# Gate and up of 18 of 22 column tiles by seven products of halves instead of eight, in both FFNs of an encoder block

## The chip, the cores and the metric

The kernel runs on one core of one Trainium2 chip. The metric is the device time of one execution in microseconds, as the median of several runs. A core has TensorE (PE, matrix products; PEld is its weight load), VectorE (DVE), ScalarE (ACT), GpSimd (POOL) and SyncE (SP, which issues the DMAs here). They run side by side, each in its own order, and wait for each other by semaphores.

## The reference, cut to what matters

One encoder block on 512 tokens and 16 meta tokens (528 rows) of width 1024: a SwiGLU FFN, a mixing stage (a gated linear recurrence beside attention), and a second SwiGLU FFN on the 512 tokens that are left.

```python
def swiglu(x, w_gate, w_up, w_down):
    return (jax.nn.silu(x @ w_gate) * (x @ w_up)) @ w_down
...
h = h + 0.5 * swiglu(rms_norm(h, ffn1_norm), ffn1_w_gate, ffn1_w_up, ffn1_w_down)
...   # mixing
h = h + 0.5 * swiglu(rms_norm(h, ffn2_norm), ffn2_w_gate, ffn2_w_up, ffn2_w_down)
```

The inner width of both FFNs is 2816, which is 22 column tiles of 128. All of it is float32.

## The kernel before, in words

Everything is held transposed: a tile has 128 features on the partitions and the tokens along the free dimension. `h` is 8 such tiles (width 1024). A float32 operand of a big product is split in two parts of the type float32r, `hi` (a rounded copy, made by ACT) and `lo` (the rest, made by a DVE subtraction), and a product is three matmuls: hi·hi, hi·lo, lo·hi (`group`, line 143). One matmul has a 128x128 block of weights as its stationary side and up to 512 tokens as its moving side.

`Weights` (line 51) brings the weights in the order of one long plan. `emit` loads one block (128x1024, 512 KB) by a DMA from SP, and writes `whi` (ACT, line 75) and `wlo` (DVE, line 76). There are two buffers of `raw`, two of `whi` and two of `wlo`; `fill` has at most three blocks traced ahead of the one that PE uses.

`ffn` (line 254) goes through the column tiles in three groups of 8, 8 and 6. For each tile it makes the gate and the up product over all 8 blocks of the width; DVE multiplies both by `R`, the reciprocal root of the mean square of each token (lines 265 and 268), which comes late in FFN1; ACT takes the silu (266), DVE multiplies (269), and ACT and DVE split the result into `hh` and `hl` (220 and 221). At the end of a group come eight "down" products of the group's tiles, each added to one tile of `h` (283). In FFN1 the 528 tokens go as 256 and 272 into two PSUM banks, in FFN2 as 512 into one; `parts` (197) deals the banks `mm` (three), `at`, `am` and the wide `S` in turn. The moving side of gate and up is `xt`, the 8 tiles of `h` times the norm's gain, split into `xh` and `xl`.

Outside of the mixing stage a planner orders the instructions of each engine: of those whose inputs and buffers its own model has ready, the one traced first goes first. A tile's buffer is taken again when the last reader of the old content is done. `gap` (208) puts unused bytes between tiles, which moves the addresses of those after it.

## Time and profile before

| | us |
|---|---|
| median of 3 runs (1236.92 to 1238.35) | 1238.31 |
| the profiled execution | 1237.46 |
| its span, first to last instruction | 1235.6 |
| PE busy | 1205.9 (98%) |
| DVE busy | 679.7 (55%) |
| ACT busy | 438.5 (35%) |
| POOL busy | 135.0 (11%) |
| mean granted clock of TensorE, of full speed | 0.994 |

FFN1 takes the span up to about 399 us, the mixing stage up to about 878 us, FFN2 the rest. Busy times of an engine are the time in which it had an instruction in work; matmuls are pipelined, so their ends are modelled and the durations of one matmul overlap those of the next. The pace of PE is read from the time that a row of equal matmuls took.

### The profile page before, as it was taken

To read this page: it belongs to the slowest core of one execution; us is meant where nothing else is said; L and a number is where in the kernel's file an instruction comes from. 1 tells how busy PE (TensorE), PEld (TensorE's weight loads), DVE (VectorE), ACT (ScalarE), POOL (GpSimd) and SP (SyncE) were. 2 spreads that over 40 slices of the span, in tenths; PEclk is the share of its full clock that TensorE was granted. 3 is DMA by queue.
4 is the path that set the end of the run, shared out by engine and by line. 5 is a ranking of instruction groups with operands and counts; after the bars stand their busy time and mean duration, and the time that the engine had idled before them with its cause. 6 is when DMAs were issued, how large, how long until landed. Compare 5 with 4: busy or idle time off the path is not lost.

```text
span 1235.6 us, 17678 instructions
## 1 busy us (share of the span) xinstructions
PE 1205.9 (98%) x7333; PEld 1078.1 (87%) x7333; DVE 679.7 (55%) x1082; ACT 438.5 (35%) x650; POOL 135.0 (11%) x122
## 2 busy tenths in 40 slices
PE   8999999999999998989889999999999999999998
PEld 8999999999999887878778788888888888888887
DVE  6544344433455879888698845454544334443443
ACT  5322122312235464555436533334323223222321
POOL 1000000000002114333142410122000000000000
PEclk9999999999999999999999999999999999999999
DMA  4232232223323311102111113233232332332223
GB/s 175 86 99 90 86 104 99 88 86 90 99 70 102 102 59 52 54 27 69 32 55 36 52 52 100 89 117 96 95 102 86 102 95 93 102 102 89 99 86 119
DMA packets 31919, 106.09 MB, mean 86 GB/s; under 512 B 3680, under 2 KB 4064, under 8 KB 31840
## 3 DMA queue, kind: packets, MB, share of 16 engines
q1 hardware_dynamic: 31680, 104.44, 26.6%
q8 instruction: 57, 0.93, 0.3%
q0 software_dynamic: 160, 0.54, 0.1%
q14 instruction: 22, 0.18, 0.0%
HBM read 102.87 MB, written 2.10 MB: 85 GB/s over the span
## 4 chain that ended last, share of the span: by engine, by line
PE 89%; DVE 7%; issue 1%; ACT 1%; DMA 0%; POOL 0%; SPq 0%; DVEq 0%; ACTq 0%; POOLq 0%
PE mm L151 49%; PE am L151 11%; PE at L151 11%; PE S L151 10%; PE gs L699 2%; PE mm L753 1%; PE mm L547 1%; PE S L509 1%; PE at L532 1%; DVE Z L688 1%; DVE aq L374 0%; DVE nm L513 0%; DVE wlo L76 0%; DVE pl L536 0%; DMA h<-in_xT 0%
## 5 line engine op out<-in xcount | busy, mean ns | idle before, releaser
L75 ACT CAST whi<-raw 128x1024 fp32r<-128x1024 f32 (+2 forms) x204 | 202.8, 994 | 571.1 <-PE mm L151 257.1
L151 PE MATMUL mm<-xh,whi 128*128 128x512 f32 (+1 forms) x872 | 270.9, 349 | 7.5 <-DVE tm L358 2.2
L151 PE MATMUL mm<-xh,wlo 128*128 128x512 f32 (+1 forms) x872 | 264.2, 342 | 0.3 <-DVE wlo L76 0.3
L151 PE MATMUL mm<-xl,whi 128*128 128x512 f32 (+1 forms) x872 | 263.6, 341 | 0.4 <-DVE xl L227 0.3
L76 DVE TENSOR_TENSOR wlo<-raw,whi 128x1024 fp32r<-128x1024 f32 (+2 forms) x204 | 235.3, 1154 | 27.6 <-ACT whi L75 22.7
L151 PEld LDWEIGHTS mm<-xh,whi 128*128 128x128 f32 x872 | 152.4, 190 | 26.7 <-DVE tm L358 2.6
L151 PEld LDWEIGHTS mm<-xh,wlo 128*128 128x128 f32 x872 | 151.7, 189 | 19.4 <-DVE wlo L76 0.8
L151 PEld LDWEIGHTS mm<-xl,whi 128*128 128x128 f32 x872 | 151.9, 189 | 16.3 <-DVE xl L227 0.8
L151 PE MATMUL mm<-hl,whi 128*128 128x512 f32 (+1 forms) x212 | 64.0, 340 | 0.1
L151 PE MATMUL mm<-hh,whi 128*128 128x512 f32 (+1 forms) x212 | 63.9, 339 | 0.0
L151 PE MATMUL mm<-hh,wlo 128*128 128x512 f32 (+1 forms) x212 | 63.9, 339 | 0.0
L686 POOL TENSOR_TENSOR Z<-Z,tot 128x512 f32<-128x512 f32 x32 | 46.2, 1442 | 152.8 <-PE gs L699 123.2
L151 PE MATMUL at<-xl,whi 128*128 128x256 f32 (+1 forms) x192 | 62.5, 326 | 0.0
L151 PE MATMUL at<-xh,wlo 128*128 128x256 f32 (+1 forms) x192 | 62.5, 326 | 0.0
L151 PE MATMUL at<-xh,whi 128*128 128x256 f32 (+1 forms) x192 | 62.5, 326 | 0.0
L151 PE MATMUL am<-xl,whi 128*128 128x272 f32 (+1 forms) x184 | 60.6, 329 | 0.0
L151 PE MATMUL am<-xh,wlo 128*128 128x272 f32 (+1 forms) x184 | 60.2, 327 | 0.0
L151 PE MATMUL am<-xh,whi 128*128 128x272 f32 (+1 forms) x184 | 60.1, 327 | 0.0
L283 DVE SCALAR_TENSOR_TENSOR h<-mm,h 128x512 f32<-128x512 f32 (+2 forms) x29 | 15.8, 565 | 64.5 <-PE mm L151 64.5
L268 DVE TENSOR_TENSOR u<-mm,R 128x512 f32<-128x512 f32 (+2 forms) x28 | 14.5, 541 | 63.8 <-PE mm L151 63.8
L151 PE MATMUL S<-xh,whi 128*128 128x256 f32 x224 | 45.8, 285 | 0.0
L238 POOL TENSOR_TENSOR acc<-acc,sq 128x528 f32<-128x528 f32 (+1 forms) x12 | 19.3, 1609 | 242.6 <-ACT sq L236 242.6
(255 smaller groups left out, 2267.5 us busy)
## 6 DMA issues: line engine op xcount, KB each, us to landing
raw<-in_wg SPq DMA_DIRECT2D x43, 512.0 KB, 3.5
raw<-in_wu SPq DMA_DIRECT2D x43, 512.0 KB, 3.5
raw<-in_w_in SPq DMA_DIRECT2D x42, 512.0 KB, 3.6
raw<-in_wd SPq DMA_DIRECT2D x32, 512.0 KB, 3.6
raw<-in_wd SPq DMA_DIRECT2D x16, 384.0 KB, 3.1
raw<-in_wup SPq DMA_DIRECT2D x16, 256.0 KB, 2.8
raw<-in_wout SPq DMA_DIRECT2D x8, 512.0 KB, 3.5
h<-in_xT SPq DMA_DIRECT2D x4, 528.0 KB, 6.1
```

The costliest lines, as they stand in the source:

```text
L75: nc.scalar.copy(hi[:, c], raw[:, c])
L76: nc.vector.tensor_tensor(lo[:, c], raw[:, c], hi[:, c].bitcast(F32), ALU.subtract)
L151: pe.matmul(o, a[:, sl], b[:, cols], start=(k == 0 and i == 0), stop=(k == n - 1 and i == 2))
L238: eng.tensor_tensor(acc[:, :n], acc[:, :n], sq[:, :n], ALU.add)
L268: dve.tensor_tensor(u[:, c], o, R[:, c], ALU.mult)
L283: dve.scalar_tensor_tensor(h[c][:, cols], o, 0.5, h[c][:, cols], ALU.mult, ALU.add)
L509: pe.matmul(s[:, WIDE][:, cols], st[e][:, c * P:(c + 1) * P], kk[:, cols], start=(i == 0), stop=(i == 1))
L532: pe.transpose(o[:, k, :], pr[:, k * P:(k + 1) * P], ident)
L547: pe.matmul(av, v[:, k, :], p[:, k, :], start=(k == 0 and i == 0), stop=False)
L686: pool.tensor_tensor(xx, xx, first, ALU.mult)
L688: dve.tensor_tensor(y, y, second, ALU.mult)
L699: pe.matmul(s[:, c, :], ks[:, c * P:(c + 1) * P], ap(Z, T + c * P, ((2 * m, P // (2 * m)), (T + m, 2), (1, m))), start=True, stop=True)
```

## The change

The columns are taken in groups of 4, 6, 6 and 6. The first group (`PLAIN`, 4 tiles) stays as it was. In the other three the tiles go in pairs (`pair`): two column tiles, two halves of the width (four blocks of 128 each) and two halves of the tokens (264 in FFN1, 256 in FFN2) make a 2x2 by 2x2 block product, for gate (i = 0) and up (i = 1), and each is done with seven products of halves. One product of halves is 4 blocks x 3 parts = 12 matmuls of 264 or 256 tokens. Sums of weight halves are made on DVE and POOL (`seven`), sums of the halves of the normed input once for each FFN (`normal`: `early` behind each tile of the first group, `late` behind the last). Products are summed in PSUM (`X`: P1+P6+P7+P4, `Z`: P5+P3) and, where one sum is used twice, in SBUF. Since `R` is in the input now, the outputs of `pair` aren't multiplied by it.

`W.extra` is the FFN's own pool: it has three more buffers of `raw`, two of `sums`, and two each of `whi` and `wlo` for the blocks of `sums` and `last`; those of `first` and `more` use the old two. The seven blocks of a pair reach `pair` in the order gate and up of `first`, of `sums`, of `more`, and `last`. `hh` and `hl` have 7 buffers instead of 10 (544 wide instead of 640 in FFN1), `g` and `u` 3 instead of 2; the buffers of the squares at the two norms take the tags of `g` and `u` in FFN1; the gaps beside `hh` are gone. `late` writes into the buffers of `xt`. The planned place of `masks` is 14 instead of 30. The mixing stage is not touched.

```diff
-GAP_X, GAP_H1, GAP_H2, GAP_Y, GAP_M = 288, 128, 0, 0, 128
+GAP_X, GAP_Y, GAP_M = 288, 0, 128
-GROUPS = ((0, 8), (8, 16), (16, 22))
+GROUPS = ((0, 4), (4, 10), (10, 16), (16, 22))
+PLAIN = 4
...
-        nc, src = self.nc, self.todo.pop(0)
-        n = src.shape[-1]
+        src = self.todo.pop(0)
+        if callable(src):
+            src()
+            return
+        nc, n = self.nc, src.shape[-1]
...
+    def parted(self, pool, pieces):
+        nc = self.nc
+        hi = pool.tile([P, 1024], F32R, name="whi", tag="whi", bufs=2)
+        lo = pool.tile([P, 1024], F32R, name="wlo", tag="wlo", bufs=2)
+        for c, src in pieces:
+            nc.scalar.copy(hi[:, c], src)
+            nc.vector.tensor_tensor(lo[:, c], src, hi[:, c].bitcast(F32), ALU.subtract)
         self.ready.append((hi, lo))
+    def seven(self, tiles):
+        nc, add, st = self.nc, self.nc.vector.tensor_tensor, {}
+        E, F = slice(0, 512), slice(512, 1024)
+        def load(key, where, bufs):
+            st[key] = where.tile([P, 1024], F32, name="raw", tag="raw", bufs=bufs)
+            nc.sync.dma_start(out=st[key], in_=tiles[key])
+        def first(i):
+            if not i:
+                load(0, self.pool, 2)
+                load(2, self.pool, 2)
+            self.parted(self.pool, [(slice(0, 1024), st[2 * i])])
+        def sums(i):
+            if not i:
+                load(1, self.extra, 3)
+                load(3, self.extra, 3)
+            t, r0, r1 = self.extra.tile([P, 1024], F32, name="sums", tag="sums", bufs=2), st[2 * i], st[2 * i + 1]
+            st["s", i] = t
+            add(t[:, E], r1[:, E], r1[:, F], ALU.add)
+            add(t[:, F], t[:, E], r0[:, E], ALU.add)
+            self.parted(self.extra, [(slice(0, 1024), t)])
+        def more(i):
+            t, r0, r1 = st["s", i], st[2 * i], st[2 * i + 1]
+            nc.gpsimd.tensor_tensor(t[:, E], r0[:, E], r1[:, E], ALU.add)
+            add(t[:, F], t[:, F], r0[:, F], ALU.add)
+            self.parted(self.pool, [(slice(0, 1024), t)])
+        def last():
+            self.parted(self.extra, [(E, st[1][:, F]), (F, st[3][:, F])])
+        return [lambda i=i, f=f: f(i) for f in (first, sums, more) for i in range(2)] + [last]
...
+        def ffn_plan(wg, wu, wd):
+            plan = []
+            for a, b in GROUPS:
+                if b <= PLAIN:
+                    for j in range(a, b):
+                        plan += [wg[j], wu[j]]
+                else:
+                    for j in range(a, b, 2):
+                        plan += W.seven([wg[j], wg[j + 1], wu[j], wu[j + 1]])
+                plan += [wd[c][:, a * P:b * P] for c in range(KT)]
+            return plan
...
+        def normal(ft, xt, gain, n):
+            nh = n // 2
+            E, F = slice(0, nh), slice(nh, n)
+            xn = ft.tile([P, KT, n], F32, name="xn", tag="xn")
+            parts_of = {}
+            def new(name, pool_t, tags):
+                parts_of[name] = tuple(pool_t(t) for t in tags)
+            def unit(t):
+                return ft.tile([P, 4, nh], F32R, name=t, tag=t)
+            def both(name, kk, src):
+                hi, lo = (t[:, kk, :] for t in parts_of[name])
+                act.copy(hi, src)
+                dve.tensor_tensor(lo, src, hi.bitcast(F32), ALU.subtract)
+            def early(kk):
+                if not kk:
+                    for nm in ("b11", "b21", "n1", "n2"):
+                        new(nm, unit, (nm + "h", nm + "l"))
+                for k in (kk, kk + 4):
+                    dve.scalar_tensor_tensor(xn[:, k], h[k][:, :n], par[:, gain + k:gain + k + 1], R[:, :n],
+                                             ALU.mult, ALU.mult)
+                u, v = xn[:, kk], xn[:, kk + 4]
+                t = ft.tile([P, 2, nh], F32, name="xm", tag="xm", bufs=1)
+                dve.tensor_tensor(t[:, 0], u[:, E], u[:, F], ALU.subtract)
+                dve.tensor_tensor(t[:, 1], t[:, 0], v[:, F], ALU.add)
+                dve.tensor_scalar(t[:, 1], t[:, 1], -1.0, None, ALU.mult)
+                both("b11", kk, u[:, E])
+                both("b21", kk, v[:, E])
+                both("n1", kk, t[:, 0])
+                both("n2", kk, t[:, 1])
+            def late():
+                room = [sp.tile([P, 4, 4, nh], F32R, name=m, tag=m) for m in ("xh", "xl")]
+                for i, nm in enumerate(("t3", "b22", "t4")):
+                    parts_of[nm] = tuple(r[:, i] for r in room)
+                for kk in range(4):
+                    u, v = xn[:, kk], xn[:, kk + 4]
+                    t = ft.tile([P, 2, nh], F32, name="xm", tag="xm", bufs=1)
+                    dve.tensor_tensor(t[:, 0], v[:, F], u[:, F], ALU.subtract)
+                    dve.tensor_tensor(t[:, 1], t[:, 0], u[:, E], ALU.add)
+                    dve.tensor_tensor(t[:, 1], t[:, 1], v[:, E], ALU.subtract)
+                    both("t3", kk, t[:, 0])
+                    both("b22", kk, v[:, F])
+                    both("t4", kk, t[:, 1])
+            return parts_of, early, late
+        def pair(ft, xq, n):
+            nh = n // 2
+            E, F = slice(0, nh), slice(nh, n)
+            banks = [[bank(t)[:, :nh] for t in ts] for ts in (("mm", "mm", "mm"), ("at", "am", "gs"))]
+            tiles = [[ft.tile([P, TP], F32, name=t, tag=t, bufs=3)[:, :n] for _ in range(2)] for t in ("g", "u")]
+            def product(o, w, half, name, start):
+                hi, lo = w
+                xh, xl = xq[name]
+                for kk in range(4):
+                    sl = slice(half * 512 + kk * P, half * 512 + (kk + 1) * P)
+                    for i, (a, b) in enumerate(((hi, xh), (hi, xl), (lo, xh))):
+                        pe.matmul(o, a[:, sl], b[:, kk, :], start=(start and kk == 0 and i == 0),
+                                  stop=(kk == 3 and i == 2), skip_group_check=True)
+            def step(i, w, half, what):
+                X, Y, Z = banks[i]
+                t0, t1 = tiles[i]
+                g0, g1 = tiles[0]
+                if what == "P1":
+                    product(X, w, half, "b11", True)
+                    act.copy(t0[:, E], X)
+                elif what == "P2":
+                    product(Y, w, half, "b21", True)
+                    dve.tensor_tensor(t0[:, E], t0[:, E], Y, ALU.add)
+                elif what == "P5":
+                    product(Z, w, half, "n1", True)
+                    act.copy(t1[:, F], Z)
+                elif what == "P6":
+                    product(X, w, half, "n2", False)
+                    act.copy(t0[:, F], X)
+                elif what == "P7":
+                    product(X, w, half, "t3", False)
+                    dve.tensor_tensor(t1[:, F], t1[:, F], X, ALU.add)
+                    if i:
+                        dve.scalar_tensor_tensor(t1[:, F], t1[:, F], -1.0, g1[:, F], ALU.mult, ALU.mult)
+                    else:
+                        act.activation(t1[:, F], t1[:, F], AF.Silu, scale=-1.0)
+                elif what == "P3":
+                    product(Z, w, half, "b22", False)
+                    dve.tensor_tensor(t0[:, F], t0[:, F], Z, ALU.add)
+                    if i:
+                        dve.tensor_tensor(t0, t0, g0, ALU.mult)
+                    else:
+                        act.activation(t0, t0, AF.Silu)
+                else:
+                    product(X, w, half, "t4", False)
+                    if i:
+                        dve.scalar_tensor_tensor(t1[:, E], X, -1.0, g1[:, E], ALU.mult, ALU.mult)
+                    else:
+                        act.activation(t1[:, E], X, AF.Silu, scale=-1.0)
+            for i in range(2):
+                w = W.next()
+                step(i, w, 0, "P1")
+                step(i, w, 1, "P2")
+            for i in range(2):
+                w = W.next()
+                step(i, w, 0, "P5")
+                step(i, w, 1, "P6")
+            ws = []
+            for i in range(2):
+                ws.append(W.next())
+                step(i, ws[i], 0, "P7")
+            for i in range(2):
+                step(i, ws[i], 1, "P3")
+            w = W.next()
+            for i in range(2):
+                step(i, w, i, "P4")
+            return tiles[1]
+        def ffn(ft, xt, gain, n, last):
+            def hidden(u):
+                hh, hl = (ft.tile([P, TP if n == T else SEQ], F32R, name=m, tag=m, bufs=7)[:, :n] for m in ("hh", "hl"))
+                split((hh, hl), u, slice(0, n))
+                return hh, hl
+            xq, early, late = normal(ft, xt, gain, n)
             for a, b in GROUPS:
                 h1 = []
-                for j in range(a, b):
+                for j in range(a, b) if b <= PLAIN else ():
                     pg = parts(n)
                     group(pg, W.next(), xt)
                     pu = parts(n)
                     group(pu, W.next(), xt)
-                    g = ft.tile([P, TP], F32, name="g", tag="g", bufs=2)[:, :T]
-                    u = ft.tile([P, TP], F32, name="u", tag="u", bufs=2)[:, :T]
+                    g, u = (ft.tile([P, TP], F32, name=t, tag=t, bufs=3)[:, :T] for t in ("g", "u"))
                     for o, c in pg:
                         dve.tensor_tensor(g[:, c], o, R[:, c], ALU.mult)
                     act.activation(g[:, :n], g[:, :n], AF.Silu)
                     for o, c in pu:
                         dve.tensor_tensor(u[:, c], o, R[:, c], ALU.mult)
                     dve.tensor_tensor(u[:, :n], u[:, :n], g[:, :n], ALU.mult)
-                    if not j:
-                        gap(ft, GAP_H1 if n == T else GAP_H2)
-                    hh, hl = (ft.tile([P, TX if n == T else SEQ], F32R, name=m, tag=m, bufs=10)[:, :n]
-                              for m in ("hh", "hl"))
-                    split((hh, hl), u, slice(0, n))
-                    h1.append((hh, hl))
+                    h1.append(hidden(u))
+                    early(j)
+                if b <= PLAIN:
+                    late()
+                for j in range(a, b, 2) if b > PLAIN else ():
+                    for u in pair(ft, xq, n):
+                        h1.append(hidden(u))
                 for c in range(KT):
...
```

## Rows read from the trace of the kernel before

**Rows 1.** The page: busy time by engine; the chain's shares; a DMA's issues, us to landing.
```profile
PE 1205.9 (98%) x7333; PEld 1078.1 (87%) x7333; DVE 679.7 (55%) x1082; ACT 438.5 (35%) x650; POOL 135.0 (11%) x122
...
PE 89%; DVE 7%; issue 1%; ACT 1%; DMA 0%; POOL 0%; SPq 0%; DVEq 0%; ACTq 0%; POOLq 0%
...
raw<-in_wg SPq DMA_DIRECT2D x43, 512.0 KB, 3.5
```

**Rows 2.** Stretch, us; busy PE, PEld, DVE, ACT, POOL (instructions); clock, DMA share, GB/s.
```profile
8.20:55.10 46.90, 46.52 (x360) 45.73 (x360) 31.86 (x42) 23.16 (x34) 4.41 (x3) 0.96 0.34 117
...
199.00:358.00 159.00, 159.00 (x1305) 159.00 (x1304) 67.26 (x103) 40.81 (x47) 0.00 (x0) 1.00 0.29 89
...
965.00:1200.00 235.00, 235.00 (x1039) 194.58 (x1038) 98.56 (x114) 61.66 (x71) 0.00 (x0) 1.00 0.31 96
```

**Rows 3.** Chain of waits in order of time: start, us, what (xmatmuls).
```profile
46.95 5.86 PE mm L151 x48
...
900.02 5.44 PE am L151 x24
...
1227.95 2.15 PE at L151 x18
```

**Rows 4.** DVE's groups, FFN1, 24 to 372: busy us, mean ns of one | idle before.
```profile
L76 DVE TENSOR_TENSOR wlo<-raw,whi 128x1024 fp32r<-128x1024 f32 x57 | 69.8, 1224 | 7.7 <-ACT whi L75 6.0
...
L221 DVE TENSOR_TENSOR hl<-u,hh 128x528 fp32r<-128x528 f32 x22 | 15.5, 704 | 4.9 <-ACT hh L220 4.9
...
L265 DVE TENSOR_TENSOR g<-mm,R 128x256 f32<-128x256 f32 x8 | 3.4, 425 | 15.0 <-PE mm L151 15.0
```

**Rows 5.** DVE's groups, FFN2, 876 to 1203.
```profile
L269 DVE TENSOR_TENSOR u<-u,g 128x512 f32<-128x512 f32 x22 | 15.2, 692 | 2.5 <-ACT whi L75 0.5
L221 DVE TENSOR_TENSOR hl<-u,hh 128x512 fp32r<-128x512 f32 x22 | 15.1, 686 | 0.7 <-ACT hh L220 0.7
```

**Rows 6.** DVE in order of time, 105 to 109, a group's last tile: start, us, what.
```profile
105.42 0.77 DVE L268 TENSOR_TENSOR u<-mm,R 128x256 f32<-128x256 f32 x2 [3.62 <-PE mm L151]
106.30 0.71 DVE L269 TENSOR_TENSOR u<-u,g 128x528 f32<-128x528 f32 x1
106.92 1.22 DVE L76 TENSOR_TENSOR wlo<-raw,whi 128x1024 fp32r<-128x1024 f32 x1
108.06 0.70 DVE L221 TENSOR_TENSOR hl<-u,hh 128x528 fp32r<-128x528 f32 x1
```

**Rows 7.** ACT's groups, FFN1, 24 to 372, then the mixing stage, 398 to 742.
```profile
L75 ACT CAST whi<-raw 128x1024 fp32r<-128x1024 f32 x56 | 59.0, 1054 | 223.8 <-PE mm L151 70.7 <-PE S L151 66.2 <-PE am L151 43.9
L266 ACT ACTIVATE g<-g 128x528 f32<-128x528 f32 x22 | 14.1, 643 | 0.1
...
L535 ACT CAST ph<-at 128x512 fp32r<-128x512 f32 x32 | 18.7, 585 | 9.6 <-PE at L532 5.3 <-PE mm L547 4.2
...
L761 ACT ACTIVATE on<-mm,yo 128x128 f32<-128x128 f32 x16 | 4.7, 367 | 7.6 <-DVE ss L755 4.8 <-DVE yo L375 2.8
```

**Rows 8.** POOL's group in the mixing stage; then single additions in order of time.
```profile
L686 POOL TENSOR_TENSOR Z<-Z,tot 128x512 f32<-128x512 f32 x32 | 46.2, 1442 | 152.8 <-PE gs L699 123.2 <-PE gs L710 14.3 <-DVE pl L536 8.1
...
379.01 1.32 POOL L238 TENSOR_TENSOR acc<-acc,sq 128x528 f32<-128x528 f32 x1 [3.12 <-ACT sq L236]
...
841.35 1.79 POOL L238 TENSOR_TENSOR acc<-acc,sq 128x512 f32<-128x512 f32 x1 [10.90 <-ACT sq L236]
```

**Rows 9.** DVE in order of time, beside the last of those additions.
```profile
841.25 0.75 DVE L227 SCALAR_TENSOR_TENSOR xl<-h,par,xh 128x512 fp32r<-128x512 f32 x1
```

**Rows 10.** DVE in order of time at 25, where R is made.
```profile
24.95 3.45 DVE L252 RECIPROCAL R<-R 128x528 f32<-128x528 f32 x1 [0.69 <-ACT R L251]
```

**Rows 11.** Line 151 on PE, 800 to 840: ns min/median/max of one.
```profile
L151 PE MATMUL mm<-xh,whi x25: 389/389/392, 799.9 to 824.6; 128*128 128x512 f32 x25
...
L151 PE MATMUL mm<-yal,whi x16: 387/395/398, 800.8 to 827.6; 128*128 128x512 f32 x16
```

More of the change, by code (lines that the diff above doesn't have):

```diff
@@ L56, in __init__ @@
         self.todo, self.ready = [], []
-        self.plain = self.into = None
+        self.plain = self.into = self.extra = None
     def plan(self, blocks):
@@ L71, in emit @@
             return
-        hi = self.pool.tile([P, 1024], F32R, name="whi", tag="whi", bufs=2)
-        lo = self.pool.tile([P, 1024], F32R, name="wlo", tag="wlo", bufs=2)
-        for c in cuts:
-            nc.scalar.copy(hi[:, c], raw[:, c])
-            nc.vector.tensor_tensor(lo[:, c], raw[:, c], hi[:, c].bitcast(F32), ALU.subtract)
-        self.ready.append((hi, lo))
+        self.parted(self.pool, [(c, raw[:, c]) for c in cuts])
+    def parted(self, pool, pieces):
[5 more added lines that the diff above has]
+            nc.vector.tensor_tensor(lo[:, c], src, hi[:, c].bitcast(F32), ALU.subtract)
+        self.ready.append((hi, lo))
+    def seven(self, tiles):
[26 more added lines that the diff above has]
+        return [lambda i=i, f=f: f(i) for f in (first, sums, more) for i in range(2)] + [last]
     def fill(self):
@@ L158, in block_kernel @@
         W = Weights(nc, wp, 2)
-        plan = []
-        for a, b in GROUPS:
-            for j in range(a, b):
-                plan += [wg1[j], wu1[j]]
-            plan += [wd1[c][:, a * P:b * P] for c in range(KT)]
-        plan.insert(30, masks)
-        W.plan(plan)
+        def ffn_plan(wg, wu, wd):
[9 more added lines that the diff above has]
+            return plan
         def const(name, src, shape, eng):
@@ L227, in gained, with squares @@
             dve.scalar_tensor_tensor(xt[1], src, g, xt[0].bitcast(F32), ALU.mult, ALU.subtract)
-        def squares(pool_t, k, n):
+        def squares(pool_t, k, n, tags):
             nonlocal acc
             if k == 0:
-                acc = pool_t.tile([P, TP], F32, name="acc", tag="acc")
+                acc = pool_t.tile([P, TP], F32, name="acc", tag=tags[0], bufs=tags[2])
                 act.activation(acc[:, :n], h[k][:, :n], AF.Square)
             else:
-                sq = pool_t.tile([P, TP], F32, name="sq", tag="sq", bufs=2)
+                sq = pool_t.tile([P, TP], F32, name="sq", tag=tags[1], bufs=tags[2])
                 act.activation(sq[:, :n], h[k][:, :n], AF.Square)
@@ L238, in squares, with normed @@
                 eng.tensor_tensor(acc[:, :n], acc[:, :n], sq[:, :n], ALU.add)
-        def normed(pool_t, k, xt, gain, n):
+        def normed(pool_t, k, xt, gain, n, tags):
             gained(k, [t[:, :n] for t in xt], h[k][:, :n], gain)
-            squares(pool_t, k, n)
+            squares(pool_t, k, n, tags)
             if k == 3:
@@ L252, in rstd @@
             dve.reciprocal(R[:, :n], R[:, :n])
-        def ffn(ft, xt, n, last):
+        def normal(ft, xt, gain, n):
[41 more added lines that the diff above has]
+            return parts_of, early, late
@@ L255, in ffn @@
+        def ffn(ft, xt, gain, n, last):
[4 more added lines that the diff above has]
+            xq, early, late = normal(ft, xt, gain, n)
             for a, b in GROUPS:
                 h1 = []
-                for j in range(a, b):
+                for j in range(a, b) if b <= PLAIN else ():
                     pg = parts(n)
@@ L290, in block_kernel @@
             xt = xtiles()
+            W.extra = ft
+            plan = ffn_plan(wg1, wu1, wd1)
+            plan.insert(14, masks)
+            W.plan(plan)
             dummy = ft.tile([P, 32], F32, name="dummy", tag="dummy")
@@ L305, in block_kernel @@
                 gained(k, xt[k], h[k], C_FFN1)
-            sums = [ft.tile([P, TP], F32, name=n, tag=n)[:, :T] for n in ("acc", "acc2")]
+            sums = [ft.tile([P, TP], F32, name=n, tag=n, bufs=3)[:, :T] for n in "gu"]
             for k in range(KT):
                 a = sums[k % 2]
-                sq = a if k < 2 else ft.tile([P, TP], F32, name="sq", tag="sq", bufs=2)[:, :T]
+                sq = a if k < 2 else ft.tile([P, TP], F32, name="sq", tag="g" if k % 2 else "u", bufs=3)[:, :T]
                 act.activation(sq, h[k], AF.Square)
@@ L334, in block_kernel @@
             plan += [wout[c] for c in range(KT)]
-            for a, b in GROUPS:
-                for j in range(a, b):
-                    plan += [wg2[j], wu2[j]]
-                plan += [wd2[c][:, a * P:b * P] for c in range(KT)]
-            W.plan(plan)
-            ffn(ft, xt, T, last1)
+            W.plan(plan + ffn_plan(wg2, wu2, wd2))
+            ffn(ft, xt, C_FFN1, T, last1)
         with tc.tile_pool(name="mix", bufs=1) as mp, tc.manual_schedule(engines={pe.engine}):
```

7 lines of the change are left out of this document (4 added, 3 removed).

## The prediction, made before the change was run

> **What bounds the kernel now.** I read the page first: PE is busy 98% of the span, and the chain that ended last lies on PE for 89% of it [rows 1]. That share mixes three stages, so next comes the table by stretch: in both FFNs PE is busy for the whole of a long stretch at the full clock, while DVE is busy 42% of it and ACT 26% [rows 2]. The chain in order of time then shows that nothing but matmuls follows nothing but matmuls there, and gives PE's pace: 48 matmuls of 256 and 272 tokens in 5.86 us (122.1 ns each), 24 of 512 in 5.44 us (226.7 ns), 18 of 256 in 2.15 us (119.4 ns) [rows 3]. So in the FFNs a matmul that is left out is time saved, as long as DVE and ACT can follow.
>
> **The change, part by part. PE.** A pair of column tiles takes gate and up of two tiles. In FFN1 that was 4 x 5.86 = 23.44 us; it becomes 14 products of 12 matmuls, 168 x 122.1 ns = 20.51 us: 2.93 us less, 26.4 us for nine pairs. In FFN2 it was 4 x 5.44 = 21.76 us; the tokens are cut in halves, so 168 matmuls of 256 at 119.4 ns take 20.06 us: 1.70 us less, 15.3 us for nine pairs. An eighth of the columns goes, but FFN2 gets more and shorter matmuls, and the rows have some 12 ns on each that is not columns; so it gains little more than half of what FFN1 does. The down products and the first four tiles have as many matmuls as before. Together 41.7 us.
>
> The Trainium skill ("TensorE: Matmul & The Clock Gate", section "Back-to-back issue gap") gives a warm matmul N/2.4 + 2.5 ns, which is an estimated 109.2 ns for 256 tokens and 215.8 ns for 512. By it FFN2 would gain 9 x (96 x 215.8 - 168 x 109.2 ns) = 21.3 us. The row at 256 [rows 3] has ten ns more, so the trace does not agree and decides.
>
> **DVE in a pair.** It makes the low part of six blocks of 1024 and of two of 512, six sums of 512, eight passes over 264 (P2, P7 and P3 of gate and up, and two products for up), one product of 528 and two low parts of 528. By whole durations that is 6 x 1.224 [rows 4] + 2 x 0.686 + 6 x 0.692 [rows 5] + 8 x 0.433 + 3 x 0.705 (from 425 ns at 256 and 704 at 528 [rows 4]) = 18.4 us. Back to back the next one starts earlier: 0.62 us after one of 528 and 1.14 us after one of 1024 [rows 6], by the line through both 0.60 for 512 and 0.34 for 264; that makes 16.2 us. FFN2 has 0.1 us less. So DVE goes from 42% to between 79% and 90% of 20.5 us, still under PE. I take it as covered by PE on the mean.
>
> **ACT in a pair.** Seven blocks' worth of casts at 1.054, six copies of 264 out of PSUM between 0.367 and 0.585 (I take 0.45, between both in width), a silu of 528 at 0.643 and two of half that (0.45), two casts of 528 at 0.64 [rows 7]: 13 us of 20.5. Covered. **POOL** has two sums of 512, 1.3 to 1.8 us each [rows 8], with 8 us between the buffers' release and use. **SP**: a pair loads the same four blocks, and there are eight more, smaller blocks of the down weights for each FFN. The next pair's first loads wait until `more` has read the old blocks, about halfway through a pair; behind them on SP's queue are only later blocks, and a block lands in 3.5 us [rows 1]. Eight more evictions of `h` for each FFN lie beside down products, where DVE is mostly idle. I cost all these at nothing; without that cover, the evictions alone would be 8 x 0.77 us [rows 6] for each FFN.
>
> **Where PE will wait all the same.** Four places; none is in the trace of before.
>
> First, the last tile of the group of four. Its low part is ready 3.3 us after its last product (DVE from 105.42 to 108.76 [rows 6]). With eight tiles PE needs it after 44 matmuls of the down product; with four after 20, 2.4 us. That is 0.9 us late; with a short new DVE instruction in front 1.2. I take 1.0 for each FFN, 2.0 (0 to 4).
>
> Second, the first down products, where `late` is also done. Low and high by the two ways of counting: `late` 24 passes of 264, 8.2 to 10.4 us; 16 evictions 5.5 to 6.9; six low parts of 512, 3.6 to 4.1; the last tile 1.9 to 2.2; the first pair's blocks 3.5 to 3.8: 22.7 to 27.4 us in PE's 23.4 (FFN1; 21.8 in FFN2). In FFN1 `early` adds 14.6 to 17.8 us (for each of four, two passes of 528 and seven of 264) to a stretch where DVE is idle for 15.0 us [rows 2], part of it before `R` is there at 28.4 us [rows 10]; some 5 us spill over. `late` is traced ahead of these down products' blocks, so DVE takes it first wherever it is ready, and PE has only two blocks in hand (5.9 us). Bounds 0 to 9 us in FFN1, 0 to 5.6 in FFN2. I take 3.5 and 1.0: gaps in `late` while ACT casts let a waiting block in, as the row at 106.92 shows one slipping into such a gap [rows 6].
>
> Third, entering each of the six groups of pairs: the second block takes the buffer of the last down block, and PE uses it 24 matmuls later (2.93 us), while eviction (0.77), cast (1.05) and low part (1.22) need 3.05. I take 0.5 each, 3.0 (0 to 7.8, with another pass of 1.2 in front).
>
> Fourth, inside a pair: up's P7 adds onto the bank that ACT must have copied after up's P6, one product (1.47 us) earlier; one cast in front makes 1.05 + 0.45 = 1.50. The same holds for the next pair's P1 behind the silu of gate's P4. I take 0.3 for each pair, 5.4 (0 to 2.1 a pair, a second cast in front of both).
>
> Waits: 2.0 + 4.5 + 3.0 + 5.4 = 14.9 us. The profiled execution was 1237.46, so 1237.46 - 41.7 + 14.9 = 1210.7; the median of before is 0.85 above that execution, which makes **1211.5 us**.
>
> **Rivals.** *All hidden.* The planner puts the copies and blocks where they are in time; only the first wait and 1.5 us are left: 1237.46 - 41.7 + 3.5 + 0.85 = 1200.1. For it: every one of the windows above misses by tenths only. Against it: DVE's 23 to 27 us in the first down products.
>
> *DVE becomes the bound through POOL.* A sum on POOL beside a DVE pass with two inputs took 1.79 us at 841.35, against 1.32 at 379.01 in a wider form [rows 8]; the DVE pass beside it, begun 0.1 us earlier, took 0.75 [rows 9], against 0.69 for passes of 512 in FFN2 [rows 5]. Here POOL lost, and DVE hardly. If DVE lost each time, a pair would cost it 18.4 + 2 x 1.442 [rows 8] = 21.3 us (21.2 in FFN2), more than PE. Then the pairs gain 9 x 2.1 + 9 x 0.6 = 24.3 us, and with 9.5 us of the first three waits it is 1237.46 - 24.3 + 9.5 + 0.85 = 1223.5. The Trainium skill ("SBUF — State Buffer", section "Who interferes with whom") has this as a rule: a DVE instruction with two SBUF inputs and a GpSimd instruction that reads SBUF exclude each other for a whole instruction, and whichever came second waits. The longer POOL sum agrees; no row of before has DVE as the second.
>
> *Slower matmuls by address.* Beside each other in one stretch, 512 tokens took 389 ns from `xh` and 395 from `yal`, with the same weight buffers [rows 11]. All moving sides of the pairs are new tiles, and the gap is gone. At 6 ns for each of 3024 matmuls: 18 us on top of the forecast, 1229.6. Against it: most tiles in the table have the lower figure.
>
> *Slower: ACT blocked by its own order.* A cast of `sums` or `more` waits for sums on DVE or POOL, and ACT takes nothing past it. If up's copy of P6 stands behind such a cast, it comes after POOL's sum 1.44, a low part 1.22, the cast 1.05 and itself 0.45, so PE waits 4.16 - 1.47 = 2.7 us in each pair: 18 x 2.7 = 48.6, and 1237.46 - 41.7 + 9.5 + 48.6 + 0.85 = 1254.7. It decides from 1.8 us a pair (32.2 / 18). For it: ACT and DVE are bound to each other in each block, and DVE has little room. Against it: the casts' inputs are ready several products before use.
>
> **How the numbers follow.** Forecast 0.43, its own range 1203 to 1220; all hidden 0.22; DVE bound 0.13; address 0.08; ACT's order 0.14, of which 0.03 ends near the old time. Faster by over 0.2% (2.5 us, about what a measurement of this kernel can tell from no change): the first four cases, 0.86. Within 0.2%: 0.03. Slower: 0.11. The range 1198 to 1233 leaves out ACT's order and the low edge of "all hidden".
>
> **What would show it.** 168 matmuls of a pair at 122 ns in FFN1 and 119 in FFN2 (the 41.7); PE idle at the first down product behind DVE's `hl` (first wait), in the next ones behind `wlo` or `h` (second), at P1 of a group behind `wlo` (third), at P7 behind ACT's copy (fourth). DVE at 80 to 90% of the pairs. The prediction fails if PE's idle time in a pair is over 1.8 us, if DVE is busy all through the pairs, or if a matmul of the pairs takes more than 125 ns.

## The result and the profile after

The changed kernel takes 1204.69 us (median of 4 runs, 1201.75 to 1208.05) against 1238.32 us before: a ratio of 0.9732 [0.9703, 0.9761], 33.6 us less. The forecast was 1211.5 us, 26.8 us less. The measured time lies in its range and in the forecast's own range, but 6.8 us below the forecast's point and 4.6 us above the rival "all hidden". The profiled execution took 1206.21 us, with a span of 1204.4.

The page of the changed kernel, busy time by engine and the chain's shares, which answers to [rows 1]:

```profile
PE 1172.3 (97%) x7765; PEld 1074.0 (89%) x7765; DVE 879.4 (73%) x1440; ACT 554.2 (46%) x920; POOL 195.2 (16%) x158
...
PE 85%; DVE 10%; issue 2%; ACT 2%; DMA 0%; POOL 0%; SPq 0%; ACTq 0%; DVEq 0%; POOLq 0%
```

PE has 432 instructions more and is busy 33.6 us less, DVE is busy 200 us more. The chain is still PE's, but 10% of it is DVE's now, for 7% before: PE waits for DVE somewhat more.

The stretches are compared by marks that both traces have. In the chain of waits in order of time (start, us, what) the second of two whole tiles of `z`, the mixing stage's first products, ends FFN1. First the kernel before, then the changed one, where `group` is line 197:

```profile
403.37 7.70 PE mm L151 x56
```
```profile
381.42 7.70 PE mm L197 x56
```

The first matmul of the norm ahead of FFN2 (the timeline of PE: start, us, what) divides the mixing stage from FFN2, again before and then changed:

```profile
875.29 1.12 PE L250 MATMUL gs<-acc,ones 128*128 128x512 f32 x2
```
```profile
855.82 1.12 PE L302 MATMUL gs<-acc,ones 128*128 128x512 f32 x2
```

| stretch, us | before | after | difference | matmuls left out, by the forecast | so waits and the like | forecast |
|---|---|---|---|---|---|---|
| FFN1, to 403.37 / 381.42 | 403.4 | 381.4 | -21.95 | -26.4 | 4.45 | 8.7 |
| mixing, to 875.29 / 855.82 | 471.9 | 474.4 | +2.5 | 0 | | 0 |
| FFN2, to the span's end | 360.3 | 348.6 | -11.7 | -15.3 | 3.6 | 6.2 |

The two FFNs together give 33.65 us, the whole difference of the medians, and what they lose is 8.05 us, not 14.9. By the same marks they lose 8.7 us in each of two later runs of the changed kernel (after_again and after_beside below). The 2.5 us of the mixing stage belong to this one execution. The same 100 us of that stage, in the table by stretch (as in [rows 2]), first before, then changed, then in a later run of a kernel with the same mixing stage (sum_on_dve below):

```profile
572.00:672.00 100.00, 90.12 (x587) 79.90 (x587) 83.14 (x164) 49.76 (x92) 31.54 (x30) 0.98 0.14 44
```
```profile
550.00:650.00 100.00, 92.06 (x573) 81.29 (x572) 81.11 (x161) 50.11 (x92) 31.57 (x30) 0.95 0.12 43
```
```profile
547.70:647.70 100.00, 90.13 (x599) 79.90 (x599) 83.36 (x164) 50.40 (x97) 31.54 (x30) 1.00 0.15 48
```

The last column but two is the granted clock: 0.98, 0.95 and 1.00 for the same work, and the stage takes 471.9, 474.4 and 470.7 us. Over the twelve runs below it was between 470.6 and 475.6, with one FFN changed, both or none (470.6 in the kernel before with halved tokens, 470.7 with FFN1 changed, 475.4 and 470.6 with both). So it is no doing of the change, and its 5 us are near the spread of the changed kernel's four times (1201.75 to 1208.05).

**The pairs.** Two stretches of a pair's length in the table by stretch of the changed kernel, one of FFN1 and one of FFN2:

```profile
104.60:125.40 20.80, 20.80 (x171) 20.62 (x170) 19.30 (x27) 12.07 (x21) 2.95 (x2) 1.00 0.30 105
1034.00:1054.20 20.20, 20.20 (x170) 20.14 (x169) 18.19 (x26) 11.63 (x19) 3.52 (x2) 1.00 0.31 104
```

PE is never idle there, at the full clock; DVE, which was busy 42% of the time in [rows 2], is busy 90 to 93%, ACT 58%. The chain in order of time shows a pair of FFN1 and one of FFN2, with 12 matmuls to a product:

```profile
104.66 2.91 PE mm L374 x24
107.57 1.60 PE at L374 x12
...
113.56 1.48 PE gs L374 x12
...
116.51 1.44 PE mm L374 x12
117.95 1.61 PE at L374 x12
...
125.40 2.91 PE mm L374 x24
...
925.86 2.88 PE mm L374 x24
...
933.05 1.59 PE at L374 x12
...
946.16 2.88 PE mm L374 x24
```

From 104.66 to the same product at 125.40 is 20.74 us for 168 matmuls, and from 925.86 to 946.16 it is 20.30. A product takes 1.44 to 1.48 us, in FFN2 1.44 (120.0 ns a matmul, for 119.4 in the forecast). In 11 of the 18 pairs one product takes 1.55 to 1.61 and in one pair two; in the third pair of each group none does. All but one of these products are up's P7, which is where the forecast's fourth wait would stand.

### The profile page after: what moved, and what is told of

Same layout as the page of the kernel before. It is cut to its first block, busy times and chain, and to the rows that moved or that the text cites. A ratio compares the mean times of both kernels' runs of the same rounds, so it can differ in the third digit from the quotient of the medians.

```text
span 1204.4 us, 19449 instructions
## 1 busy us (share of the span) xinstructions
PE 1172.3 (97%) x7765; PEld 1074.0 (89%) x7765; DVE 879.4 (73%) x1440; ACT 554.2 (46%) x920; POOL 195.2 (16%) x158
## 4 chain that ended last, share of the span: by engine, by line
PE 85%; DVE 10%; issue 2%; ACT 2%; DMA 0%; POOL 0%; SPq 0%; ACTq 0%; DVEq 0%; POOLq 0%
PE mm L197 34%; PE mm L374 14%; PE at L374 9%; PE at L197 5%; PE am L197 5%; PE gs L374 4%; PE S L197 4%; PE am L374 2%; PE gs L884 2%; DVE wlo L85 2%; PE mm L938 1%; PE mm L732 1%; PE S L694 1%; PE at L717 1%; ACT whi L84 1%
## 5 line engine op out<-in xcount | busy, mean ns | idle before, releaser
L197 PE MATMUL mm<-xh,whi 128*128 128x512 f32 (+1 forms) x504 | 166.8, 364 | 9.9 <-DVE tm L543 2.3
L197 PE MATMUL mm<-xl,whi 128*128 128x512 f32 (+1 forms) x504 | 160.0, 351 | 0.4 <-DVE xl L279 0.3
L197 PE MATMUL mm<-xh,wlo 128*128 128x512 f32 (+1 forms) x504 | 159.2, 349 | 0.3 <-DVE wlo L85 0.3
L197 PEld LDWEIGHTS mm<-xh,whi 128*128 128x128 f32 x504 | 89.8, 191 | 23.2 <-DVE tm L543 2.7
L85 DVE TENSOR_TENSOR wlo<-sums,whi 128x1024 fp32r<-128x1024 f32 x72 | 87.6, 1218 | 24.9 <-ACT whi L84 24.7
L84 ACT CAST whi<-sums 128x1024 fp32r<-128x1024 f32 x72 | 75.4, 1051 | 62.6 <-DVE sums L111 21.0
L197 PEld LDWEIGHTS mm<-xh,wlo 128*128 128x128 f32 x504 | 89.1, 190 | 13.4 <-DVE wlo L85 0.8
L197 PE MATMUL mm<-hh,whi 128*128 128x256 f32 (+1 forms) x218 | 62.9, 333 | 0.1
L197 PE MATMUL mm<-hh,wlo 128*128 128x256 f32 (+1 forms) x218 | 63.0, 334 | 0.0
L197 PE MATMUL mm<-hl,whi 128*128 128x256 f32 (+1 forms) x218 | 62.9, 332 | 0.0
L884 PEld LDWEIGHTS gs<-Z,ks 128*128 128x128 f32 x224 | 30.6, 198 | 12.8 <-issue 7.3
```

The source lines that it names most:

```text
L84: nc.scalar.copy(hi[:, c], src)
L85: nc.vector.tensor_tensor(lo[:, c], src, hi[:, c].bitcast(F32), ALU.subtract)
L197: pe.matmul(o, a[:, sl], b[:, cols], start=(k == 0 and i == 0), stop=(k == n - 1 and i == 2))
L884: pe.matmul(s[:, c, :], ks[:, c * P:(c + 1) * P], ap(Z, T + c * P, ((2 * m, P // (2 * m)), (T + m, 2), (1, m))), start=True, stop=True)
```

## The experiments

Two halves of the change, each alone, ask whether the gain is PE's count of matmuls and adds up.

**ffn1_only, ffn2_only.** The other FFN has the groups of 8, 8 and 6 and eight products.

```diff
+OLD = ((0, 8), (8, 16), (16, 22)), 22
...   # ffn and ffn_plan take the groups and the number of plain tiles
# ffn1_only
-            ffn(ft, xt2, C_FFN2, SEQ, last2)
+            ffn(ft, xt2, C_FFN2, SEQ, last2, *OLD)
# ffn2_only
-            ffn(ft, xt, C_FFN1, T, last1)
+            ffn(ft, xt, C_FFN1, T, last1, *OLD)
...   # in both, the plan of that FFN's weights gets *OLD too
```

> Seven products in FFN1 alone; FFN2 as before. Theory (the gain of each FFN is its own matmuls at the measured pace, less small waits of its own, and the two gains add): FFN1 came out 22 us shorter in the profiled execution, so 1238.3 - 22 = about 1216. Forecast's own waits (8.7 us in FFN1): 1238.3 - 26.4 + 8.7 = 1220.6. Rival (the mixing stage, 2.5 us longer in the profiled execution after the change, is longer because of what FFN1 leaves behind): 1218.8, with a mixing stage of 474 to 475 us instead of 472.

> Seven products in FFN2 alone; FFN1 as before. Theory: FFN2 came out 11.7 us shorter, so about 1226.6, with a mixing stage of 472 us. Forecast's own waits (6.2 us in FFN2): 1238.3 - 15.3 + 6.2 = 1229.2.

Measured: 1218.11 us, 0.9828 [0.9803, 0.9853], and 1227.3 us, 0.9901 [0.9874, 0.9928], with 1239.47 for the kernel before on that chip: 21.4 and 12.2 us less. Together 33.5 us, as much as the whole change: the parts add, within the some 3 us that each interval leaves on either side, and no cost that the two FFNs share is to be seen. Both are near what the theories gave (22 and 11.7 us less). By the forecast's own waits it would have been 17.7 and 9.1; the first lies outside the measured interval, the second just within. The rival's mixing stage of 474 to 475 us didn't come: it took 470.7 us with FFN1 changed alone.

**pe_as_written.** PE does its instructions in the order in which the program writes them; the planner orders the other engines as before.

```diff
-            ffn(ft, xt, C_FFN1, T, last1)
+            with tc.manual_schedule(engines={pe.engine}):
+                ffn(ft, xt, C_FFN1, T, last1)
...   # and the same around the FFN2 call
```

> The changed kernel with PE's instructions of both FFNs in the order in which they are written, instead of the planner's. Theory (the forecast's waits are real for a PE that goes in written order, and the planner hid 7 of the 14.9 us by giving PE other matmuls that were ready): 1204.7 + 7 = about 1212, with PE idle at hl of the last of the four tiles, and at wlo where a group of pairs begins. Rival (the waits were mis-sized, the order on PE has nothing to do with it): 1204.7 within 2 us.

Measured: 1207.69 us, 0.9745 [0.9721, 0.977], which overlaps the changed kernel's interval. The first wait is there, in both FFNs (timeline of PE; in brackets the idle time before and what ended it):

```profile
64.13 0.51 PE L197 MATMUL S<-hh,whi 128*128 128x256 f32 x2 [0.71 <-ACT hh L272]
64.88 0.51 PE L197 MATMUL S<-hl,whi 128*128 128x256 f32 x2 [0.23 <-DVE hl L273]
...
899.76 0.50 PE L197 MATMUL am<-hh,whi 128*128 128x512 f32 x1 [0.85 <-ACT hh L272]
900.49 0.50 PE L197 MATMUL am<-hl,whi 128*128 128x512 f32 x1 [0.23 <-DVE hl L273]
```

0.94 and 1.08 us, where the forecast had 1.0 for each. In the changed kernel it is gone, and its timeline at that place shows how:

```profile
62.15 0.28 PE L197 MATMUL mm<-hl,whi 128*128 128x256 f32 x1
62.35 0.51 PE L197 MATMUL S<-hh,whi 128*128 128x256 f32 x2
62.70 0.28 PE L197 MATMUL mm<-hl,whi 128*128 128x272 f32 x1
```

PE has begun the second down product (in `mm`) while the first (in `S`) still lacks the fourth tile, and takes the matmuls of that tile up in between. Two waits more appear in the written order, one in each FFN: at the first down product behind a group of pairs PE waits 0.6 us for DVE's pass behind up's P4. The second wait's largest piece (0.6 us in FFN1) is gone instead. So the planner's order of PE is worth the first wait at most, and the 1212 us expected by the forecast's sizes were not reached.

**before_halves.** The kernel before, but gate and up of FFN2 as two halves of 256 tokens: as many columns, twice the matmuls.

```diff
-                    pg = parts(n)
+                    pg = halves(n)     # FFN2: two banks of 256
...
-                    pu = parts(n)
+                    pu = halves(n)
```

> The kernel before, with gate and up of FFN2 as two matmuls of 256 tokens for each of 512: 1056 matmuls become 2112, same columns. Theory (some 12 ns of each matmul are not columns): 1056 x (2 x 119.4 - 226.7 ns) = 12.8 us more, 1251. Rival (2.5 ns for each matmul beside its columns): 1056 x 2.5 ns = 2.6 us more, 1241.

Measured: 1254.33 us, 1.0122 [1.0095, 1.015]. FFN2 is 15.1 us longer (375.4 us by the marks above, for 360.3). Its pace in the chain:

```profile
1014.83 5.76 PE mm L151 x48
```

120.0 ns a matmul, so two of 256 cost 240.0 ns where one of 512 cost 226.7 [rows 3]: 13.3 x 1056 = 14.0 us of the 15.1, for 12.8 expected by the theory and 2.6 by the rival. The part of a matmul that is not columns is real, and it is why FFN2 gained about half of what FFN1 did.

**sum_on_dve, p3_behind_p7, after_again.** The sum of `more` on DVE takes POOL's lock away and gives DVE more work. P3 put right behind P7 for gate and then for up puts two products instead of one between up's P6 and its P7. The changed kernel ran beside them once more.

```diff
# sum_on_dve
-            nc.gpsimd.tensor_tensor(t[:, E], r0[:, E], r1[:, E], ALU.add)
+            add(t[:, E], r0[:, E], r1[:, E], ALU.add)
# p3_behind_p7
-            ws = []
-            for i in range(2):
-                ws.append(W.next())
-                step(i, ws[i], 0, "P7")
             for i in range(2):
-                step(i, ws[i], 1, "P3")
+                w = W.next()
+                step(i, w, 0, "P7")
+                step(i, w, 1, "P3")
```

> The sum of more that POOL makes is made by DVE instead: POOL does nothing in a pair, DVE has two more passes of 512. Theory (DVE's passes beside POOL's sum are stretched, 1.79 us instead of 0.69 at 108.99 in the changed kernel's trace, but PE doesn't wait for DVE in the pairs): the stretched passes go, DVE's busy time in a middle pair stays within 1 us of 18.7, the time stays at 1204.7 within 2.5 us. Rival (DVE is the bound of the pairs through POOL): faster by over 10 us. Other rival (DVE has no room for 1.2 us more): slower by about 9 x 2 x 1 = 18 us.

> The order of products is gate P7, gate P3, up P7, up P3 instead of gate P7, up P7, gate P3, up P3, so that two products lie between up's P6 and up's P7 and ACT has twice the time to copy the bank. Theory (a pair loses 0.14 us at up's P7, seen as 12 matmuls in 1.61 instead of 1.47 us): that loss goes from each pair, 18 x 0.14 = 2.5 us faster than the changed kernel, 1202. Rival (the loss moves to up's P3 or to another bank): 1204.7 within 1 us, with a longer row of 12 elsewhere.

> The changed kernel again, beside the three others on the same chip, to compare them with it. All theories: ratio 0.973 to the kernel before within 0.003; the mixing stage between 470 and 475 us whatever the FFNs do.

Measured: 1202.28 us, 0.9717 [0.9691, 0.9743]; 1207.42, 0.9755 [0.9732, 0.9778]; the changed kernel 1206.36, 0.9735 [0.9711, 0.9759]. All three intervals overlap. The lock that the rival spoke of, by which a DVE pass with two inputs in SBUF and a POOL operation wait for one another, is there. In the changed kernel one POOL sum and the DVE pass beside it, each in its own engine's timeline:

```profile
108.59 1.65 POOL L116 TENSOR_TENSOR sums<-raw 128x512 f32<-128x512 f32 x1 [9.10 <-DVE wlo L85]
```
```profile
108.99 1.79 DVE L117 TENSOR_TENSOR sums<-sums,raw 128x512 f32<-128x512 f32 x1
```

And by groups of DVE in FFN1's pairs, 85 to 380 (as in [rows 4]), the changed kernel and then sum_on_dve:

```profile
L85 DVE TENSOR_TENSOR wlo<-raw,whi 128x1024 fp32r<-128x1024 f32 x19 | 26.4, 1390 | 0.5 <-ACT whi L84 0.2
L117 DVE TENSOR_TENSOR sums<-sums,raw 128x512 f32<-128x512 f32 x18 | 19.7, 1095 | 0.0
L110 DVE TENSOR_TENSOR sums<-raw 128x512 f32<-128x512 f32 x16 | 15.2, 951 | 2.7 <-DMA raw<-in_wu 2.5
```
```profile
L85 DVE TENSOR_TENSOR wlo<-raw,whi 128x1024 fp32r<-128x1024 f32 x19 | 23.2, 1223 | 1.2 <-ACT whi L84 0.2
L117 DVE TENSOR_TENSOR sums<-sums,raw 128x512 f32<-128x512 f32 x18 | 12.3, 685 | 0.0
...
L110 DVE TENSOR_TENSOR sums<-raw 128x512 f32<-128x512 f32 x16 | 11.0, 685 | 0.1
```

Here DVE is the one that waits: a pass of 512 takes 1095 ns in the mean instead of 685, and these three groups lose 3.2 + 7.4 + 4.2 = 14.8 us in nine pairs. Inside the pairs PE does not notice, because DVE keeps 7 to 10% of a pair. Giving DVE 18 sums more, 685 ns each as in L117's row (12.3 us), and taking 14.8 us of lock away comes out about even.

Where PE enters a group of pairs, it does notice. In the changed kernel at FFN1's second group (timelines of POOL, DVE and PE), and then the same pass in sum_on_dve:

```profile
182.58 1.31 POOL L116 TENSOR_TENSOR sums<-raw 128x512 f32<-128x512 f32 x1 [4.16 <-DVE wlo L85]
182.70 2.27 DVE L85 TENSOR_TENSOR wlo<-raw,whi 128x1024 fp32r<-128x1024 f32 x1
185.03 0.39 PE L374 MATMUL at<-b11h,wlo 128*128 128x264 f32 x1 [0.66 <-DVE wlo L85]
```
```profile
181.73 1.22 DVE L85 TENSOR_TENSOR wlo<-raw,whi 128x1024 fp32r<-128x1024 f32 x1
```

The low part begins 0.12 us after POOL's sum and takes 2.27 us instead of 1.22, and PE idles for it. The third group has the same (0.71 us idle). In both runs of sum_on_dve PE waits at neither of these two entries. From FFN1's first matmul into `mm` behind 28 us to the norm that ends it, and from the norm of FFN2 to the span's end, they together take 3.7 us (sum_on_dve) and 3.0 us (sum_on_dve_again, below) less than the changed kernel's run beside each. The medians differ by 4.1 us less and 0.2 us more, which the 5 us of the mixing stage can hide or make up; so the lock's price, 1.9 us at these two entries and at most some 3 us in all, is read from traces and not from the times. (1.4 of the 3.7 us are at FFN1's first entry, which varies between executions; see below.)

For p3_behind_p7 up's P7 lost its wait, but not enough of it for a time. PE's waits in FFN1's pairs (what it waited for, us in total, times, longest) in after_again, then p3_behind_p7, and up's P7 in the latter's chain:

```profile
PE at L374 <- DVE wlo L85: 1.6, 3, 0.7
PE at L374 <- ACT whi L84: 0.9, 1, 0.9
```
```profile
PE at L374 <- DVE wlo L85: 1.7, 3, 0.7
PE at L374 <- ACT whi L84: 0.8, 1, 0.8
...
120.22 1.44 PE at L374 x12
```

Nothing moved elsewhere: the two lists are alike. Up's P7 takes as long as other products in ten of the twelve pairs where it was longer, and 0.3 us more in the first pair of each FFN. By the starts of PE's matmuls that is some 0.9 us less in all, which these medians can't tell from nothing. The 2.5 us expected had 0.14 us in all 18 pairs.

Both lists have a wait that the profiled execution of the changed kernel hasn't: ACT's cast of the second block, at FFN1's first entry. It waits for that block's load, here in the chain of after_again (4.82 us in after_beside; in the profiled execution such a load landed after 3.3 us):

```profile
79.82 4.72 DMA raw<-in_wu
```

**four_sums_on_pool.** Three further POOL sums beside each one of `more`, into a buffer that nobody reads: does the lock have a price once DVE's room is used up?

```diff
             nc.gpsimd.tensor_tensor(t[:, E], r0[:, E], r1[:, E], ALU.add)
+            for _ in range(3):
+                x = self.extra.tile([P, 512], F32, name="scr", tag="scr", bufs=1)
+                nc.gpsimd.tensor_tensor(x, r0[:, E], r1[:, E], ALU.add)
```

> POOL makes the sum of more and then three further ones of the same size into a scratch tile that nobody reads: six more POOL sums in a pair. Theory (a POOL sum that runs can hold up a DVE pass with two SBUF inputs by up to about 1.1 us, and DVE has some 2 us of room in a pair): DVE's passes are stretched until it is busy all through the pairs, and PE waits; at 0.7 us for each of the six sums less 2 us of room, 2.2 us a pair, 40 us slower, 1244. Rival (POOL gives way to DVE): PE waits for nothing new, 1204.7 within 3 us.

Measured: 1301.3 us, 1.0514 [1.0491, 1.0537], far more than the 1244 expected. The stretch of FFN1's pairs, its group on DVE, and what PE waited for most:

```profile
85.00:430.00 345.00, 310.08 (x2396) 303.07 (x2397) 263.23 (x308) 136.13 (x215) 130.55 (x77) 0.97 0.25 81
...
L120 DVE TENSOR_TENSOR sums<-sums,raw 128x512 f32<-128x512 f32 x18 | 30.0, 1669 | 0.0
...
PE mm L377 <- DVE wlo L85: 15.4, 8, 3.0
```

The pass that took 1095 ns takes 1669 and PE waits for DVE. But DVE is busy only 76% of the stretch. The sums also hold the `raw` buffers longer, so loads can come later (not separated here), and the 95 us need not be the lock's alone.

**pool_sums_of_r.** The same sums of `R`, which holds no `raw`, were to leave that out.

```diff
-                nc.gpsimd.tensor_tensor(x, r0[:, E], r1[:, E], ALU.add)
+                nc.gpsimd.tensor_tensor(x, self.R[:, E], self.R[:, E], ALU.add)
```

> As the run with four sums on POOL, but the three further sums read R, so that they keep no block of weights from being loaded anew. Theory (POOL's sums hold up DVE's passes with two SBUF inputs, and this alone makes DVE the bound): DVE's passes of 1024 and 512 on SBUF are stretched as in that run, no wait for a load of weights is left, and the time is still over 1260. Rival (most of the 95 us came from the loads that had to wait for the further sums): under 1225.

Measured: 1282.62 us, 1.0356 [1.0335, 1.0377], but by another way than meant. `R` is there early, so POOL did all 54 sums of FFN1 at its start, back to back. Beside them on DVE (first line POOL, then DVE, in their timelines), and PE's stretch:

```profile
63.03 8.00 POOL L119 TENSOR_TENSOR scr<-R 128x512 f32<-128x512 f32 x5
...
64.30 0.42 DVE L453 TENSOR_TENSOR g<-am,R 128x272 f32<-128x272 f32 x1
...
66.89 1.27 DVE L339 TENSOR_TENSOR xm<-xn 128x264 f32<-128x264 f32 x1
...
85.00:105.00 20.00, 7.65 (x30) 6.42 (x30) 19.76 (x25) 4.89 (x12) 15.83 (x14) 0.50 0.04 13
```

A DVE pass with two inputs in SBUF takes 1.27 us for 264 elements, for 0.43 without POOL; one with an input in PSUM (`am`) keeps its 0.42. DVE is busy 99% of the stretch and PE 38%, at a granted clock of 0.50 (1.2 GHz) after long idle times. So the lock alone, with no loads in it, can make DVE the bound. What it costs inside the pairs is not separated by this run.

**late_behind_down, sum_on_dve_again, after_beside.** The changed kernel with `late` traced behind the first eight down products, with two repetitions beside it.

```diff
-                if b <= PLAIN:
-                    late()
...                for c in range(KT): ...   # the down products
+                if b <= PLAIN:
+                    late()
```

> late is traced behind the first eight down products instead of ahead of them, so that their blocks and evictions go first on DVE. Theory (late costs PE little where it is: the first down products of FFN1 took 24.6 us for 23.4 us of matmuls): those products take 23.5 to 24 us, and the whole is 1 to 2 us faster, or as much slower if the first pair now waits for P7's input. Forecast's second wait (4.5 us for both FFNs): 4 us faster, 1200.

> The run with the sum of more on DVE once more, with more rounds and beside the changed kernel. Theory (DVE gets back what POOL's sum took from it, 1.7 us a pair, for the 1.4 us of the sum itself, and PE's waits for low parts at the entry of the groups go): 1 to 3 us faster than the changed kernel, 1202 to 1204. Rival (no difference): ratio to before 0.9735 as the changed kernel.

> The changed kernel beside these three on the same chip. All theories: ratio to before 0.973 within 0.003.

Measured: 1203.81 us, 0.9717 [0.9695, 0.9738]; 1204.76, 0.9726 [0.971, 0.9742]; 1204.53, 0.9724 [0.9707, 0.9742]: no difference that the times show. In the table by stretch, the first down products of FFN1 and FFN2, after_beside and then late_behind_down:

```profile
57.95:82.81 24.86, 24.53 (x194) 23.83 (x193) 20.73 (x50) 11.05 (x22) 0.93 (x1) 1.00 0.38 114
893.65:916.55 22.90, 22.78 (x98) 17.72 (x96) 20.02 (x41) 10.96 (x22) 0.00 (x0) 1.00 0.34 103
```
```profile
59.30:83.12 23.82, 23.82 (x194) 23.67 (x193) 22.04 (x50) 11.15 (x22) 1.15 (x1) 1.00 0.41 120
896.44:918.57 22.13, 22.13 (x97) 17.87 (x96) 20.40 (x41) 10.97 (x22) 0.00 (x0) 1.00 0.36 107
```

`late`'s place costs PE 1.0 and 0.8 us there; matmuls alone are 192 x 122.1 ns = 23.4 and, in FFN2, 21.8 us. That is most of the second wait: 1.2 to 1.4 us and 1.1, against 3.5 and 1.0. The wait at FFN1's first entry went with it, and between the marks used for sum_on_dve the FFNs take 3.1 us less than in after_beside. The medians are 0.7 us apart, and the mixing stage of the profiled execution took 474.4 us beside 470.6, so the times don't show it.

## Why the forecast was right, and which of its terms were not

*PE's matmuls as the bound: right.* PE at the full clock without idle time in the pairs, 33.65 us from both FFNs, the two halves alone adding up to 33.5, and the halves of the kernel before for FFN2's smaller share. The 41.7 us hold but for the pace in FFN2: 120.0 ns for 119.4 makes 0.6 x 168 x 9 = 0.9 us. The formula that the prediction sets beside its rows ("TensorE: Matmul & The Clock Gate", section "Back-to-back issue gap" of the Trainium skill) stands there for a single matmul by itself. The rows are of a stream, so they were no test of it; the choice of the rows was right, as before_halves shows.

*DVE covered by PE: right inside the pairs, with less room than it looks.* 90 to 93% of a pair, where the two ways of counting had given 79 and 90. The lock of the rival has a part in it: 14.8 us in FFN1's nine pairs, 1.6 a pair. The rule quoted for that rival ("SBUF — State Buffer", section "Who interferes with whom" of the Trainium skill) is now seen with DVE as the loser: 1.79 us beside POOL's 1.65, and not for a pass with an input in PSUM, of which the same section says that a DVE instruction with at most one SBUF input, outside its two-port modes, doesn't contend. As the prediction put it, "no row of before has DVE as the second", but the trace of before had such passes: in its mixing stage, where POOL sums run among them, DVE's sums of 512 took 990 ns in the mean, against 692 of such a product in [rows 5].

```profile
L688 DVE TENSOR_TENSOR Z<-Z,tot 128x512 f32<-128x512 f32 x16 | 15.8, 990 | 7.6 <-PE gs L699 3.8 <-issue 2.3 <-PE gs L710 1.4
```

The rival failed in its last step: it charged whole POOL sums (1.442) to DVE and took whole durations for the rest (18.4), which counts as time the overlap of passes that follow each other. With starts counted (16.2) and 1.6 us of lock it is 17.8, which fits in a pair; the rows show 18.2 to 19.3 busy, so up to 1.5 us of a pair is not accounted for.

*The waits: the term that was mis-sized, 14.9 us for 8.05.* By place, in the profiled execution:

| wait | forecast, us | measured, us | shown by |
|---|---|---|---|
| first, fourth tile's `hl` | 2.0 | 0; 2.0 in the written order | pe_as_written |
| second, beside `late` | 4.5 | 2.3 | the windows; late_behind_down |
| third, entry of six groups | 3.0 | 3.1, at all six | starts of PE's matmuls; sum_on_dve |
| fourth, inside a pair | 5.4 | 1.7, in 12 pairs | the long products; p3_behind_p7 |
| FFN2's pace | 0 | 0.9 | the chain |

The first was right in size for PE in the written order; the step that failed is that the planner moves single matmuls of PE as well, not whole products. The second failed by the bounds: for `early` some 5 us were to spill over, but DVE is done with all of it before 59, and blocks slip in between `late`'s passes. In DVE's timeline of the changed kernel:

```profile
68.40 0.69 DVE L85 TENSOR_TENSOR wlo<-raw,whi 128x512 fp32r<-128x512 f32 x1
```

The third is right in total, and partly by luck. It is counted from start to start of PE's matmuls, as a list of waits leaves out short ones and the next matmul comes 0.1 us late too: 0.39, 0.93 and 0.98 us in FFN1, 0.34, 0.23 and 0.23 in FFN2. The forecast had 0.5 at each, by an eviction, a cast and a low part behind each other. The two large ones are the low part held up by POOL's sum, a price that the forecast had only in a rival, and they go with that sum. In after_again and after_beside the first entry takes 1.7 and 1.8 us instead of 0.4, behind the late load; the forecast had put loads at nothing.

The fourth is the long products of the chain, 0.11 to 0.16 us each where the forecast had 0.3 for each of 18 pairs; the one of them that is not up's P7 (107.57) is up's P1. The five rows make 8.0 us. Two more differences about cancel: FFN1 starts some 0.8 us later (`R`'s reciprocal begins at 25.74, for 24.95 in [rows 10]; it varies between executions and is not the change's), and 168 of its matmuls without a wait take 20.43 us (125.40 to 145.83 in the chain) and not 20.51, 0.7 us in nine pairs.

*The other rivals.* "All hidden" was nearest in time but not in mechanism: the wait it kept is the one that vanished, and the three that it all but dropped are there. "Slower by address": a product of the pairs takes 1.44 to 1.48 us with any of the tiles; it failed. "ACT blocked by its own order" would show 2.7 us in each pair; no product inside a pair takes more than 1.61 us, of some 1.45.

*What stays open:* how a kernel with less than these 7 to 10% of room on DVE would fare in the pairs, since neither POOL run separated it; why one load takes 3.3 us in one execution and 4.7 in another; and what moves the clock in the mixing stage from run to run.

## What to carry to other kernels

Where PE is the bound at the full clock, price an algebraic saving by matmuls at their measured pace for each width, not by columns: halving the width cost 13.3 ns a pair of matmuls, and that took 10.1 us of the 24.5 us that an eighth of FFN2's columns would have saved. Where a planner orders the tensor engine too, a wait behind one operand can be filled with other matmuls, as at the first down product; it is not where the next matmuls need the same operand, as at the entries of the groups. Count a second engine by its starts and add the lock for each overlapping POOL operation before calling it covered, and look for the place where that engine's result is needed at once.

## What the runs showed of the hardware that was not expected

DVE can be the one that loses against POOL, for as long as POOL's operation lasts: 264 elements in 1.27 us instead of 0.43 beside POOL operations that follow each other, in two-input passes from SBUF, and not in those with an input from PSUM (0.42). A low part of 1024 that began 0.12 us after a POOL sum took 2.27 us instead of 1.22, and PE waited for it. The granted clock of the same mixing stage was between 0.93 and 1.00 in its middle 100 us in different runs (0.93 in after_again, where the stage took 475.4 us; 1.00 in sum_on_dve, 470.7).
